# The RWKV stage of a hybrid backbone: TensorE's order written out by the program, dense work between the steps of preparation and none in the recurrence

## The chip, the core and the metric

The kernel runs on one core of a Trainium2 chip. The metric is the device time of one execution in microseconds (us), the median of several runs.

## The reference

Two layers work on 512 latent tokens and 256 context tokens of 1024 channels. A layer normalises and modulates its input to `u`, projects it, sends the parts through four mixers (RWKV-7, SSD, Hyena, retention), merges these under sigmoid gates and adds the output projection. Cut to what the change touches:

```python
for layer in range(2):
    need_ctx = layer < 1
    u_c, gate_c = modulate(h_ctx, cond_ctx, norm_w[layer], ada_w[layer], ada_b[layer])
    u_l, gate_l = modulate(h_lat, cond_lat, norm_w[layer], ada_w[layer], ada_b[layer])
    pc = split_in(u_c @ in_w[layer]); pl = split_in(u_l @ in_w[layer])
    ...   # per head of RWKV, token by token, in both directions, the context first:
        sa = -einsum('bhvk,bhk->bhv', s, kk_t)
        s = s * w_t[:, :, None, :] + sa[..., None] * b_t[:, :, None, :] + v_t[..., None] * k_t[:, :, None, :]
        y_t = einsum('bhvk,bhk->bhv', s, r_t)
    ...   # u, mod = cond @ ada_w + ada_b; merge: sum over m of sigmoid(u @ merge_w_m) * (ys_m @ branch_w_m)
```

The second layer needs no outputs for the context tokens.

## The kernel before

**Dense work.** A projection of 128 output channels (`dense`, L209) multiplies a weight block of 1024 x 128 with `u`. For accuracy `u` and the weights are held as a high and a low part, and three products are summed: `uh,whi`, `ul,whi`, `uh,wlo`. The tokens are cut in 512 (`dl`) and 256 (`dc`). Weights come by DMA (`wraw`), ACT casts the high part (`whi`, L185), VectorE subtracts it (`wlo`, L186), three buffers each. `stream` runs a list of such projections and parks their results in DRAM; it serves all mixers, and some of it convolves or gates on VectorE (L413, L711, L712).

**RWKV** (`rwkv`, `rwkv_ct`) goes through four blocks of 128 channels (two heads). A block has a *preparation*: an elementwise chain on VectorE, head sums, then for each direction d the matmuls `AR,KB` whose results VectorE masks into `A` (L577), the transposes of `KB` and the values to `KBt` and `vt`. Then comes the *inverse* of 48 triangular 32x32 blocks on VectorE: four transposes of `A` (L618), 60 small operations (L622, L623), six transposes (L627, L629) into `TT`. TensorE multiplies these with `A` and `late` in 32x32 pieces, and ACT copies the results into `TT`.

Then the *recurrence* goes through 12 chunks of 64 tokens, both directions in one tile. A step is: `UV,A` and `Z,AR` into one PSUM tile, an ACT copy to `Rs` (L669), `Rs,TT`, an ACT copy to `UV` (L675), `UV,KBt`, and two VectorE operations that add the old state and multiply by the decay `pcm` to the new state `Z` (L684, L685). The outputs (`AR,Z` and `A,UV` into `yl`) hang on that. GpSimd clears half of `UV` (L655), copies the values into it (L657) and makes `pcm` (L659). A group norm, the bonus and a gate end the block.

**Order.** A scheduler sets the order of every engine's queue. It takes the dense matmuls that stand after a block in the program into whatever holes it sees: they lie between the steps of the recurrence as well. TensorE's order, like every other engine's, is fixed when the program is built; an instruction that isn't ready holds up all that stand behind it.

**After RWKV** come the rest of the projections, Hyena, SSD, retention, then `merge` for each mixer. The modulation of the next layer (`ada_load`, `ada_step`, 64 weight pieces) runs eight pieces per output column inside the last merge of the first layer.

## Time and profile before

| | |
|---|---|
| median of 3 runs | 3047.11 us (3041.41 to 3059.58) |
| profiled execution | 3056.07 us, span 3054.3 us |
| TensorE busy | 2872.5 us (94%) |
| VectorE, ScalarE (ACT), GpSimd (POOL) busy | 1952.7 (64%), 1162.8 (38%), 446.8 us (15%) |
| mean granted TensorE clock | 0.968 |
| RWKV stages | 200 to 850 us and 1860 to 2515 us of the span |
| modulation of layer 2 | inside 1470 to 1655 us |

PE is TensorE, DVE is VectorE, POOL is GpSimd. Granted clock 1.00 is 2.4 GHz, 0.50 is 1.2 GHz. A matmul's time in the profile covers its run through the pipeline, so the starts of neighbours tell what one costs. An engine's idle time is charged to what ended it.

### The profile page before, as it was taken

To read this page: it belongs to the slowest core of one execution; us is meant where nothing else is said; L and a number is where in the kernel's file an instruction comes from. 1 tells how busy PE (TensorE), PEld (TensorE's weight loads), DVE (VectorE), ACT (ScalarE), POOL (GpSimd) and SP (SyncE) were. 2 spreads that over 40 slices of the span, in tenths; PEclk is the share of its full clock that TensorE was granted. 3 is DMA by queue.
4 is the path that set the end of the run, shared out by engine and by line. 5 is a ranking of instruction groups with operands and counts; after the bars stand their busy time and mean duration, and the time that the engine had idled before them with its cause. 6 is when DMAs were issued, how large, how long until landed. Compare 5 with 4: busy or idle time off the path is not lost. (4 is left out here: it accounts for less than half of the span.)

```text
span 3054.3 us, 48430 instructions
## 1 busy us (share of the span) xinstructions
PE 2872.5 (94%) x18708; PEld 2311.2 (76%) x18708; DVE 1952.7 (64%) x3576; ACT 1162.8 (38%) x2087; POOL 446.8 (15%) x650
## 2 busy tenths in 40 slices
PE   8998989999999999999998999898999999999897
PEld 3786777777788888778866868776777778877677
DVE  3469494949332778877466446959494825787865
ACT  4653243334232223344344454434252323333432
POOL 2311202020100001210120231120202020011111
PEclk9999999999999999999998979999999999999999
DMA  5642121212153332134256254323132225332334
GB/s 192 206 146 80 61 99 58 89 47 70 48 184 114 123 114 91 58 130 142 90 181 211 89 168 151 103 80 101 51 107 68 73 71 177 125 119 87 126 120 144
DMA packets 164266, 343.24 MB, mean 112 GB/s; under 512 B 19105, under 2 KB 28130, under 8 KB 164036
## 3 DMA queue, kind: packets, MB, share of 16 engines
q1 hardware_dynamic: 164036, 340.15, 33.9%
q8 instruction: 147, 2.41, 0.3%
q14 instruction: 83, 0.68, 0.1%
HBM read 254.77 MB, written 83.74 MB: 111 GB/s over the span
## 5 line engine op out<-in xcount | busy, mean ns | idle before, releaser
L209 PE MATMUL dl<-uh,wlo 128*128 128x512 f32 (+1 forms) x1520 | 620.9, 409 | 16.2 <-DVE wlo L186 16.1
L209 PE MATMUL dl<-uh,whi 128*128 128x512 f32 (+1 forms) x1520 | 620.2, 408 | 8.2 <-ACT xp L257 7.0
L209 PE MATMUL dl<-ul,whi 128*128 128x512 f32 (+1 forms) x1520 | 624.0, 411 | 2.0 <-DVE ul L363 2.0
L186 DVE TENSOR_TENSOR wlo<-wraw,whi 128x512 fp32r<-128x512 f32 x452 | 326.1, 722 | 336.9 <-ACT whi L185 298.6
L185 ACT CAST whi<-wraw 128x512 fp32r<-128x512 f32 x452 | 278.2, 616 | 628.6 <-PE dc L209 325.3
L209 PEld LDWEIGHTS dl<-uh,wlo 128*128 128x128 f32 (+1 forms) x1520 | 290.8, 191 | 82.6 <-DVE wlo L186 20.6
L209 PEld LDWEIGHTS dl<-uh,whi 128*128 128x128 f32 (+1 forms) x1520 | 290.0, 191 | 65.7 <-ACT xp L257 7.5
L209 PEld LDWEIGHTS dl<-ul,whi 128*128 128x128 f32 (+1 forms) x1520 | 290.0, 191 | 61.6 <-DVE ul L363 5.6
L209 PE MATMUL dc<-uh,whi 128*128 128x256 f32 (+1 forms) x960 | 279.0, 291 | 16.3 <-ACT xp L257 7.1
L209 PE MATMUL dc<-ul,whi 128*128 128x256 f32 (+1 forms) x960 | 276.7, 288 | 2.2 <-DVE ul L363 2.2
L209 PE MATMUL dc<-uh,wlo 128*128 128x256 f32 (+1 forms) x960 | 275.9, 287 | 0.0
L209 PEld LDWEIGHTS dc<-uh,whi 128*128 128x128 f32 (+1 forms) x960 | 182.4, 190 | 34.2 <-ACT xp L257 9.9
L209 PEld LDWEIGHTS dc<-ul,whi 128*128 128x128 f32 (+1 forms) x960 | 182.5, 190 | 19.1 <-DVE ul L363 6.2
L209 PEld LDWEIGHTS dc<-uh,wlo 128*128 128x128 f32 (+1 forms) x960 | 182.0, 190 | 3.5 <-issue 0.6
L1208 POOL TENSOR_TENSOR acc<-acc,fg 128x512 f32<-128x512 f32 x72 | 95.1, 1329 | 511.4 <-DVE fg L1207 511.4
L684 DVE TENSOR_TENSOR Z<-cc,Z 128x256 f32<-128x256 f32 x80 | 33.9, 424 | 203.9 <-PE cc L174 203.9
L655 POOL MEMSET UV<- 64x256 f32 x96 | 29.4, 306 | 674.5 <-PE yl L174 374.9
L814 POOL TENSOR_TENSOR m<-smask,adl 128x512 fp32r<-128x512 f32 x24 | 34.1, 1419 | 590.3 <-DVE adl L186 463.3
L669 ACT COPY Rs<-cc 64x256 f32<-64x256 f32 x96 | 35.2, 367 | 197.6 <-PE cc L174 196.9
L209 PE MATMUL dl<-yh,whi 128*128 128x512 f32 x256 | 103.3, 405 | 3.2 <-ACT yh L185 2.1
L209 PE MATMUL dl<-yl,whi 128*128 128x512 f32 x256 | 102.9, 404 | 3.1 <-DVE yl L186 3.1
L209 PE MATMUL dl<-yh,wlo 128*128 128x512 f32 x256 | 103.9, 407 | 0.0
(411 smaller groups left out, 5828.7 us busy)
## 6 DMA issues: line engine op xcount, KB each, us to landing
wraw<-in_w SPq DMA_DIRECT2D x248, 256.0 KB, 2.7
wraw<-merge_w SPq DMA_DIRECT2D x128, 256.0 KB, 2.8
adr<-ada_w SPq DMA_DIRECT2D x96, 256.0 KB, 3.6
wraw<-branch_w SPq DMA_DIRECT2D x64, 256.0 KB, 2.7
wraw<-out_w SPq DMA_DIRECT2D x32, 256.0 KB, 3.6
pdlw<-fg SPq DMA_DIRECT2D x16, 384.0 KB, 2.6
pdla<-fg SPq DMA_DIRECT2D x16, 384.0 KB, 2.9
hfd<-Hs SPq DMA_DIRECT2D x16, 384.0 KB, 2.3
```

The source lines that it names most:

```text
L185: (heng or self.S).copy(out=hi, in_=src) if heng is None else heng.tensor_copy(out=hi, in_=src)
L186: (leng or self.V).tensor_tensor(out=lo, in0=src, in1=hi.bitcast(F32), op=ALU.subtract)
L209: self.P.matmul(out[t0][:M, :n], w[:, kk, :], u[:, k, t0:t0 + n], start=(k == 0 and p == 0), stop=(k == nk - 1 and p == 2))
L655: G.memset(UV[hb], 0.0)
L669: S.copy(out=Rs[hb], in_=Rp.t[hb])
L684: V.tensor_tensor(out=Zn[:], in0=Zp.t[:], in1=Z[:], op=ALU.add)
L814: eng.tensor_tensor(out=m2[:], in0=self.smask[:, d, :].unsqueeze(1).to_broadcast([128, 4, 128]), in1=ad[:, c, hs:hs + 4].bitcast(F32).unsq ...
L1208: G.tensor_tensor(out=acc[:, oc, t0:t0 + n], in0=acc[:, oc, t0:t0 + n], in1=g[:, t0:t0 + n], op=ALU.add)
```

## The change

1. **TensorE's order.** The RWKV stage of both layers runs with TensorE's order as the program writes it (`manual_schedule`). `fill(us)` places dense chunks worth so many us (12 matmuls of n columns count 12 n / 2260) between steps of the preparation: 5, then 17 or 11, four times 1.6, four times 1.4, 4, 34, twice 1.4 and 4 per block, 89.8 us in all. `require` brings in what a block needs. What is left runs after the fourth block.
2. **Recurrence.** There is no dense work in it. Every step works on one direction and then the other: `Z`, `Rs`, the copy to `UV` and the state operations are half as wide and twice as many. The outputs of a step come one step later, and the products with the values (`from_v`) one step earlier. `UV` is no longer cleared.
3. **Inverse.** One transpose of all 128 partitions makes `TT`, and one makes `TB` (the tile `et`); they take the place of six of 32 partitions. Two ACT copies and two GpSimd memsets follow the first.
4. **Weights.** In the lead and RWKV stages of both layers GpSimd and not VectorE subtracts the high part (256 of 452 subtractions).
5. **Modulation.** Two pieces run per output column in all four merges of the first layer.
6. The light projections (`rv` to `zs`) now come before Hyena's, whose results are convolved on VectorE.

```diff
-    PSUM_A = dict(cc=3, yl=1, d1=1)
+    PSUM_A = dict(cc=4, yl=1)
...
-            self.split(hi[:], lo[:], raw[:])
+            self.split(hi[:], lo[:], raw[:], leng=self.wl)
         return hi, lo
...
@@ -207,6 +209,12 @@
                     k = j * 4 + kk
                     for p, (w, u) in enumerate(((hi, uh), (hi, ul), (lo, uh))):
                         self.P.matmul(out[t0][:M, :n], w[:, kk, :], u[:, k, t0:t0 + n], start=(k == 0 and p == 0), stop=(k == nk - 1 and p == 2))
+                yield 12 * n / 2260
...
-        m = self.tile(self.fpool, [n, 512], F32, "fg")
+        m = self.tile(self.apool, [n, 512], F32, "am")
         self.S.copy(out=m[:], in_=self.adps[:])
-        pc = self.ps("dc", [128, 4, 2])
+        pc = self.ps("s" if "s" in self.pb else "cc", [128, 4, 2])
...
+    def fill(self, us):
+
+        self.credit += us
+        while self.credit > 0:
+            c = next(self.feed, None)
+            if c is None:
+                return
+            self.credit -= c
+
+    def require(self, nm, j):
+        while (nm, j) not in self.parked:
+            self.credit -= next(self.feed)
+
...
+        self.feed = self.stream_steps(l, need_ctx, items)
+        self.credit = 0
         for ct in range(4):
             y, no = self.rwkv_ct(l, ct, need_ctx, pa, pb, segs, osegs)
-            self.stream(l, need_ctx, items[ct])
+            self.require("ga", ct)
...
+        for _ in self.feed:
+            pass
...
     def rwkv_ct(self, l, ct, need_ctx, pa, p, segs, osegs):
         V, S, G = self.V, self.S, self.G
+        for nm in "krv":
+            self.require(nm, ct)
...
+        self.fill(5)
...
+            self.fill(11 if d else 17)
+            nf = 0
...
                     pp = [self.ps("cc", [128, 4, 128]) for h in range(2)]
+                    nf += 1
+                    if nf > 2:
+                        self.fill(1.6)
...
             kt = self.tile(p, [128, 12, 128], F32, "KBt", bufs=2)
+            self.fill(1.4)
             for g in range(3):
...
+            self.fill(1.4)
...
+        self.fill(4)
         cb = self.headsum(ksum, osegs)
...
-        G.memset(TT[32:64, :, 0:32], 0.0)
-        G.memset(TT[96:128, :, 0:32], 0.0)
         for par in range(2):
             for blk in range(2):
...
+
+        V.transpose(out=TT[:, :, 0:32].rearrange("p u t -> p t u"), in_=B)
         for par in range(2):
-            V.transpose(out=TT[qs[par, 0], :, 32:64].rearrange("p u s -> p s u"), in_=B[qs[par, 0]].rearrange("p t s -> p s t"))
-            for blk in (1, 0):
-                V.transpose(out=TT[qs[par, blk], :, blk * 32:blk * 32 + 32].rearrange("p u t -> p t u"), in_=B[qs[par, blk]])
+            S.copy(out=TT[qs[par, 1], :, 32:64], in_=TT[qs[par, 1], :, 0:32])
+            G.memset(TT[qs[par, 1], :, 0:32], 0.0)
+        TB = self.tile(p, [128, 32, 32], F32, "et")
+        V.transpose(out=TB[:].rearrange("p u s -> p s u"), in_=B.rearrange("p t s -> p s t"))
         X = self.tile(p, [128, 24, 32], F32, "late")
+        self.fill(34)
         for d in range(2):
             ps = self.ps("cc", [128, 12, 32])
...
-                    self.mm(ps, ps.t[qs[par, 1], u, :], A[qs[par, 0], par * 24 + d * 12 + u, 32:64], TT[qs[par, 0], 8 * par + d * 12 + u, 32:64])
+                    self.mm(ps, ps.t[qs[par, 1], u, :], A[qs[par, 0], par * 24 + d * 12 + u, 32:64], TB[qs[par, 0], 8 * par + d * 12 + u, :])
...
         for d in range(2):
             ps = self.ps("cc", [128, 12, 32])
+            if d == 0:
+                self.fill(1.4)
...
+        self.fill(1.4)
         y = self.tile(p, [128, T], F32, "y")
+        Z = UVp = Yp = None
...
+        def from_v(c):
+            par = c % 2
+            hb, hk = slice(64 * (1 - par), 64 * (1 - par) + 64), slice(64 * par, 64 * par + 64)
+            ps = self.ps("cc", [128, 4, 64])
+            for d in range(2):
+                for h in range(2):
+                    self.mm(ps, ps.t[hb, d * 2 + h, :], A[hk, at(c, d, h), 0:64], vt[d][hk, [(c + 8) % 12, c][d] // 2, 64 * h:64 * h + 64])
+            return ps
+
+        def inner(c, uv):
+            for d in range(2):
+                for h in range(2):
+                    ao = A[:, at(c, d, h), 127:63:-1] if d else A[:, at(c, d, h), 64:128]
+                    self.mm(Yp, Yp.t[64 * h:64 * h + 64, nat(c, d):nat(c, d) + 64], uv[:, d, h, :], ao)
+
+        Rp = from_v(0)
         for c in range(12):
+            outs = c >= 4 or need_ctx
             if c == 4 or c == 0 and need_ctx:
...
             UV = self.tile(p, [128, 2, 2, 64], F32, "UV")
-            G.memset(UV[hb], 0.0)
             for d in range(2):
                 G.tensor_copy(out=UV[hk, d], in_=vt[d][hk, slot[d] // 2, :].rearrange("p (h x) -> p h x", h=2))
...
-            Rp = self.ps("cc", [128, 4, 64])
+            Rs = self.tile(p, [128, 4, 64], F32, "Rs")
             for d in range(2):
-                for h in range(2):
-                    idx = par * 24 + d * 12 + h * 6 + slot[d] // 2
-                    self.mm(Rp, Rp.t[hb, d * 2 + h, :], A[:, idx, 0:64], UV[:, d, h, :])
...
+                if Z is not None:
+                    self.mm(Rp, Rp.t[hb, 2 * d:2 * d + 2, :].rearrange("p h x -> p (h x)"), ar[d][:, slot[d], 0, :], Z[d][:])
+                S.copy(out=Rs[hb, 2 * d:2 * d + 2], in_=Rp.t[hb, 2 * d:2 * d + 2])
+            if outs and Z is not None:
                 for d in range(2):
-                    self.mm(Rp, Rp.t[hb, 2 * d:2 * d + 2, :].rearrange("p h x -> p (h x)"), ar[d][:, slot[d], 0, :], Z[:, d, :])
-            Rs = self.tile(p, [128, 4, 64], F32, "Rs")
-            S.copy(out=Rs[hb], in_=Rp.t[hb])
+                    self.mm(Yp, Yp.t[:, nat(c, d):nat(c, d) + 64], Z[d][:], ar[d][:, slot[d], 1, ::-1] if d else ar[d][:, slot[d], 1, :])
             Up = self.ps("cc", [128, 4, 64])
...
                     self.mm(Up, Up.t[hb, d * 2 + h, :], TT[hb, lane, :], Rs[hb, d * 2 + h, :])
-            S.activation(out=UV[hb].rearrange("p d h x -> p (d h) x"), in_=Up.t[hb], func=AF.Copy, scale=-1.0)
+                S.activation(out=UV[hb, d], in_=Up.t[hb, 2 * d:2 * d + 2], func=AF.Copy, scale=-1.0)
+            if UVp is not None:
+                inner(c - 1, UVp)
+            UVp = UV if outs else None
             if c < 11:
                 Zp = self.ps("cc", [128, 2, 128])
+                Zn = []
                 for d in range(2):
                     self.mm(Zp, Zp.t[:, d, :], kbt[d][:, slot[d], :], UV[:, d].rearrange("p h x -> p (h x)"))
-                Zn = self.tile(p, [128, 2, 128], F32, "Z")
-                if Z is None:
-                    V.tensor_tensor(out=Zn[:], in0=Zp.t[:], in1=pcm[:], op=ALU.mult)
-                else:
-                    V.tensor_tensor(out=Zn[:], in0=Zp.t[:], in1=Z[:], op=ALU.add)
-                    V.tensor_tensor(out=Zn[:], in0=Zn[:], in1=pcm[:], op=ALU.mult)
...
-                    if Z is not None:
-                        self.mm(Yp, Yp.t[:, nat:nat + 64], Z[:, d, :], rho)
...
-                        self.mm(Yp, Yp.t[hr, nat:nat + 64], UV[:, d, h, :], ao)
-            Z = Zn
...
+                    zn = self.tile(p, [128, 128], F32, f"Z{d}", bufs=2)
+                    if Z is None:
+                        V.tensor_tensor(out=zn[:], in0=Zp.t[:, d], in1=pcm[:, d], op=ALU.mult)
+                    else:
+                        V.tensor_tensor(out=zn[:], in0=Zp.t[:, d], in1=Z[d][:], op=ALU.add)
+                        V.tensor_tensor(out=zn[:], in0=zn[:], in1=pcm[:, d], op=ALU.mult)
+                    Zn.append(zn)
+                Z = Zn
+                if c == 3 and need_ctx:
+                    inner(c, UVp)
+                    UVp = None
+                    S.copy(out=y[:, 512:768], in_=Yp.t[:])
+                Rp = from_v(c + 1)
+        inner(11, UVp)
+        self.fill(4)
...
+            light = some(rv=4, rk=4, rq=4, gr=4, gh=4, zs=4)
+            items = []
+            for c in range(4):
+                items += [(n, c + 1) for n in "krv" if c < 3] + [("ga", c)] + light[6 * c:6 * c + 6]
+            items += [("hy", 4 * j + c) for c in range(4) for j in range(3)] + some(dt=1, x=4, B=2, C=2)
             adas = [(l, j, k) for l, j0 in ((0, 4), (1, 0)) for j in range(j0, 6) for k in range(8)]
...
+                self.wl = self.G
...
-                        with pool(f"ra{l}") as pa:
-                            with pool(f"rw{l}") as p:
-                                self.rwkv(l, need, pa, p, items)
                         nmg = 0 if need else 2
-                        self.stream(l, need, rest + [("mg", 24 + j) for j in range(nmg)])
+                        with tc.manual_schedule(engines={mybir.EngineType.PE}), pool(f"ra{l}") as pa, pool(f"rw{l}") as p:
+                            self.rwkv(l, need, pa, p, items + [("mg", 24 + j) for j in range(nmg)])
...
+                self.wl = self.V
...
-                    self.merge(l, 0, need, mp, acc, True)
-                    self.merge(l, 2, need, mp, acc, False)
-                    self.stream(l, need, [("mg", 24 + j) for j in range(nmg, 8)])
-                    self.merge(l, 1, need, mp, acc, False)
                     with pool(f"ada{l}") as self.apool:
-                        q = []
+                        q, todo = [], list(adas) if need else []
 
                         def each(oc):
-                            for a in adas[8 * oc:8 * oc + 8]:
-                                q.append(self.ada_load(*a))
-                                if len(q) > 2:
+                            for _ in range(2):
+                                if todo:
+                                    q.append(self.ada_load(*todo.pop(0)))
+                                if q and (len(q) > 2 or not todo):
                                     self.ada_step(*q.pop(0))
 
-                        self.merge(l, 3, need, mp, acc, False, True, each if need else None)
-                        for a in q:
-                            self.ada_step(*a)
+                        self.merge(l, 0, need, mp, acc, True, each=each)
+                        self.merge(l, 2, need, mp, acc, False, each=each)
+                        self.stream(l, need, [("mg", 24 + j) for j in range(nmg, 8)])
```

On TensorE, inside a recurrence step of the first block, this stands before (`Z,AR`, `Rs,TT` and so on as above, `dl` and `dc` dense):

```order
L174 MATMUL cc_2036<-UV_2015,KBt_1635 128x128
L174 MATMUL cc_2036<-UV_2015,KBt_1727 128x128
L174 MATMUL yl_1953<-A_1570,UV_2015 64x64 x2
L174 MATMUL yl_1953<-AR_1680,Z_2006 128x64
L174 MATMUL yl_1953<-A_1570,UV_2015 64x64 x2
L174 MATMUL cc_2054<-UV_2048,A_1570 64x64 x4
L209 MATMUL dl_4770<-uh_141,wlo_948_4805 128x512
L209 MATMUL dl_4770<-uh_141,whi_947_4804 128x512
L209 MATMUL dl_4770<-ul_142,whi_947_4804 128x512
L209 MATMUL dl_4770<-uh_141,wlo_948_4805 128x512
L209 MATMUL dc_4771<-uh_141,whi_947_4804 128x256
```

and this after, where `Z_541` and `Z_542` are the states of the two directions and `vt,A` is `from_v`:

```order
L174 MATMUL cc_2712<-vt_1892,A_1622 64x64 x2
L174 MATMUL cc_2712<-vt_2132,A_1622 64x64 x2
L174 MATMUL cc_2712<-Z_541_2707,AR_1639 64x128
L174 MATMUL cc_2712<-Z_542_2710,AR_1930 64x128
L174 MATMUL yl_2689<-AR_1639,Z_541_2707 128x64
L174 MATMUL yl_2689<-AR_1930,Z_542_2710 128x64
L174 MATMUL cc_2729<-Rs_2722,TT_2207 64x64 x4
L174 MATMUL yl_2689<-A_1622,UV_2690 64x64 x4
L174 MATMUL cc_2740<-UV_2717,KBt_1873 128x128
L174 MATMUL cc_2740<-UV_2717,KBt_2099 128x128
```

Two dense runs of four or more per step are gone, and the output products of the step before stand between `Rs,TT` and `UV,KBt`.

On TensorE, after the change, at the end of `fill(34)` in the first block (`et,A` is `TB` times `A`, the first product that needs the inverse's result):

```order
L211 MATMUL dl_2525<-uh_141,wlo_525_2530 128x512
L211 MATMUL dl_2525<-uh_141,whi_524_2529 128x512
L211 MATMUL dl_2525<-ul_142,whi_524_2529 128x512
L211 MATMUL dl_2525<-uh_141,wlo_525_2530 128x512
L174 MATMUL cc_2545<-et_2278,A_1622 32x32 x24
L174 MATMUL cc_2572<-et_2278,A_1622 32x32 x24
L211 MATMUL dc_2526<-uh_141,whi_524_2529 128x256
L211 MATMUL dc_2526<-ul_142,whi_524_2529 128x256
```

and on GpSimd, around the memset of that block's `TT`, which must wait for ACT's copy of the first transpose:

```order
L186 TENSOR_TENSOR wlo_516_2464<-wraw_514_2461,whi_515_2463 128x512
L186 TENSOR_TENSOR wlo_519_2494<-wraw_517_2491,whi_518_2493 128x512
L671 MEMSET TT_2207 32x32x32 x2
L186 TENSOR_TENSOR wlo_525_2530<-wraw_523_2527,whi_524_2529 128x512
L186 TENSOR_TENSOR wlo_532_2668<-wraw_530_2665,whi_531_2667 128x512
L186 TENSOR_TENSOR wlo_635_3143<-wraw_633_3140,whi_634_3142 128x512
```

The memset stands ahead of the subtraction for `wlo_525`, with which the last matmuls of `fill(34)` work.

On VectorE, after the change, inside the inverse of the fourth block (L663 and L664 are its small operations, L779 and L780 the convolution of a Hyena projection):

```order
L664 TENSOR_TENSOR KB_7033<-KB_7033 128x19x12
L663 TENSOR_TENSOR KB_7033<-KB_7033 128x234
L779 SCALAR_TENSOR_TENSOR fg_7150<-xp_60_157,cols_48_121,fg_7150 128x512
L664 TENSOR_TENSOR KB_7033<-KB_7033 128x18x13
L780 SCALAR_TENSOR_TENSOR fg_7150<-xp_60_157,cols_48_121,fg_7150 128x512
L663 TENSOR_TENSOR KB_7033<-KB_7033 128x238
L779 SCALAR_TENSOR_TENSOR fg_7150<-xp_60_157,cols_48_121,fg_7150 128x256
L664 TENSOR_TENSOR KB_7033<-KB_7033 128x17x14
L780 SCALAR_TENSOR_TENSOR fg_7150<-xp_60_157,cols_48_121,fg_7150 128x256
L663 TENSOR_TENSOR KB_7033<-KB_7033 128x240
L664 TENSOR_TENSOR KB_7033<-KB_7033 128x16x15
L663 TENSOR_TENSOR KB_7033<-KB_7033 128x240
```

The subtractions that stood inside the inverse are gone from VectorE; evictions of dense results stand in it as before.

## Rows read from the trace of the kernel before

**Rows 1.** Windows of both RWKV stages: start, length, busy of five engines, granted clock, DMA.

```profile
200.00:850.00 650.00, 610.52 (x4876) 492.54 (x4875) 451.04 (x775) 236.53 (x436) 98.49 (x215) 0.96 0.22 72
1860.00:2515.00 655.00, 611.88 (x4564) 479.78 (x4564) 439.40 (x754) 240.13 (x438) 102.71 (x220) 0.96 0.26 85
```

**Rows 2.** Waits of TensorE, first stage (200–850): total us, times, longest us.

```profile
PE cc L174 <- DVE TT L627: 16.9, 7, 4.6
```

**Rows 3.** Waits of TensorE, second stage (1860–2515).

```profile
PE cc L174 <- DVE TT L627: 16.8, 7, 6.0
PE dl L209 <- DVE wlo L186: 12.8, 7, 4.3
```

**Rows 4.** Windows, matmuls of line 209 alone: length, busy and count, clock.

```profile
200.00:850.00 650.00, 379.08 (x1806) 0.96 0.22 72
304.80:371.10 66.30, 29.64 (x120) 1.00 0.18 61
...
1860.00:2515.00 655.00, 398.22 (x1672) 0.96 0.26 85
...
2439.80:2501.60 61.80, 29.80 (x119) 1.00 0.15 50
```

**Rows 5.** Groups of VectorE by line, whole program: busy, mean ns.

```profile
L623 DVE TENSOR_TENSOR KB<-KB 128x30 f32<-128x30 f32 (+14 forms) x240 | 82.2, 342 | 3.6
L622 DVE TENSOR_TENSOR KB<-KB 128x30 f32<-128x30 f32 (+14 forms) x240 | 79.9, 333 | 3.9
L618 DVE STREAM_TRANSPOSE KB<-A 32x1024 f32<-32x1024 f32 x32 | 64.3, 2009 | 2.7 <-PE cc L174 2.4
L629 DVE STREAM_TRANSPOSE TT<-KB 32x1024 f32<-32x1024 f32 x32 | 62.3, 1947 | 0.9
```

**Rows 6.** Timeline of TensorE before a TT matmul: start, us, instruction, [idle <- releaser].

```profile
2293.42 0.39 PE L209 MATMUL dl<-uh,wlo 128*128 128x512 f32 x1
2293.65 0.40 PE L209 MATMUL dl<-uh,whi 128*128 128x512 f32 x1
2296.27 1.70 PE L174 MATMUL cc<-TT,A 32*32 32x32 f32 x92 [2.22 <-DVE TT L627]
```

**Rows 7.** Timeline of one recurrence step: start, us, instruction.

```profile
2470.82 0.65 PE L174 MATMUL cc<-Z,AR 128*64 128x128 f32 x4
...
2471.57 0.37 ACT L669 COPY Rs<-cc 64x256 f32<-64x256 f32 x1 [3.58 <-PE cc L174]
...
2473.92 0.61 PE L174 MATMUL cc<-UV,KBt 128*128 128x128 f32 x4
...
2474.57 0.42 DVE L684 TENSOR_TENSOR Z<-cc,Z 128x256 f32<-128x256 f32 x1 [0.61 <-PE cc L174]
...
2475.26 0.63 PE L174 MATMUL cc<-UV,A 128*64 128x64 f32 x8
```

**Rows 8.** Groups of VectorE by shape, whole program.

```profile
L577 DVE TENSOR_TENSOR A<-cc,maska 128x128 f32<-128x128 f32 x32 | 8.6, 285 | 5.8 <-PE cc L174 5.8
```

**Rows 9.** Groups of GpSimd by shape, whole program.

```profile
L814 POOL TENSOR_TENSOR m<-smask,adl 128x512 fp32r<-128x512 f32 x24 | 34.1, 1419 | 590.3 <-DVE adl L186 463.3 <-PE s L174 127.0
```

**Rows 10.** Timeline inside an inverse, VectorE and GpSimd.

```profile
275.63 0.69 DVE L186 TENSOR_TENSOR wlo<-wraw,whi 128x512 fp32r<-128x512 f32 x1
...
277.11 0.41 DVE L623 TENSOR_TENSOR KB<-KB 128x238 f32<-128x238 f32 x1
277.14 1.28 POOL L420 TENSOR_TENSOR fg<-xp 128x512 f32<-128x512 f32 x1 [9.79 <-ACT xp L257]
...
277.55 1.12 DVE L622 TENSOR_TENSOR KB<-KB 128x234 f32<-128x234 f32 x1
```

**Rows 11.** Waits of TensorE while the modulation runs (1470–1660).

```profile
PE sy L303 <- DVE adl L186: 7.4, 12, 1.3
```

**Rows 12.** Windows of all engines in three stretches.

```profile
1625.00:1660.00 35.00, 26.91 (x95) 14.76 (x96) 22.38 (x37) 21.30 (x35) 2.34 (x2) 0.66 0.68 212
2158.00:2186.00 28.00, 28.00 (x226) 18.21 (x227) 6.54 (x14) 6.83 (x16) 8.49 (x23) 1.00 0.10 30
2298.00:2311.80 13.80, 13.80 (x138) 10.66 (x139) 9.07 (x13) 5.97 (x12) 1.17 (x3) 0.51 0.38 125
```

More of the change, by code (lines that the diff above doesn't have):

```diff
@@ L196, in weights, with dense_steps @@
         with self.tc.high_priority(offset=500):
-            self.split(hi[:], lo[:], raw[:])
+            self.split(hi[:], lo[:], raw[:], leng=self.wl)
         return hi, lo
-    def dense(self, srcs, uh, ul, segs, M=128):
-        out = {t0: self.pst("dl" if n > 256 else "dc", [128, n]) for t0, n in segs}
+    def dense_steps(self, out, srcs, uh, ul, segs, M=128):
+        for t0, n in segs:
+            out[t0] = self.pst("dl" if n > 256 else "dc", [128, n])
         nk = len(srcs) * 4
@@ L209, in dense @@
                         self.P.matmul(out[t0][:M, :n], w[:, kk, :], u[:, k, t0:t0 + n], start=(k == 0 and p == 0), stop=(k == nk - 1 and p == 2))
+                yield 12 * n / 2260
+    def dense(self, srcs, uh, ul, segs, M=128):
+        out = {}
+        for _ in self.dense_steps(out, srcs, uh, ul, segs, M):
+            pass
         return out
@@ L387, in apply_gate, with stream_steps @@
         self.V.scalar_tensor_tensor(out=y[:, :no], in0=g[:, :no], scalar=0.5, in1=y[:, :no], op0=ALU.mult, op1=ALU.mult)
+    def fill(self, us):
[8 more added lines that the diff above has]
+            self.credit -= next(self.feed)
     def stream(self, l, need_ctx, items):
+        for _ in self.stream_steps(l, need_ctx, items):
+            pass
+    def stream_steps(self, l, need_ctx, items):
         V, S, G = self.V, self.S, self.G
@@ L407, in stream @@
             M = 16 if nm == "dt" else 128
-            ps = self.dense([src[:, 0:4], src[:, 4:8]], self.uh, self.ul, sg, M)
+            ps = {}
+            yield from self.dense_steps(ps, [src[:, 0:4], src[:, 4:8]], self.uh, self.ul, sg, M)
             g = fg()
@@ L697, in rwkv_ct @@
-            Z = Zn
-            if c == 3 and need_ctx:
-                S.copy(out=y[:, 512:768], in_=Yp.t[:])
+                    zn = self.tile(p, [128, 128], F32, f"Z{d}", bufs=2)
[4 more added lines that the diff above has]
+                        V.tensor_tensor(out=zn[:], in0=zn[:], in1=pcm[:, d], op=ALU.mult)
@@ L1287, in run @@
             self.cond()
-            items = [[(n, c + 1) for n in "krv"] + [("ga", c)] for c in range(3)] + [[("ga", 3)]]
             def some(**kw):
                 return [(n, j) for n, c in kw.items() for j in range(c)]
-            rest = [("hy", 4 * j + c) for c in range(4) for j in range(3)] + some(gh=4, dt=1, x=4, B=2, C=2, zs=4, rq=4, rk=4, rv=4, gr=4)
+            light = some(rv=4, rk=4, rq=4, gr=4, gh=4, zs=4)
[3 more added lines that the diff above has]
+            items += [("hy", 4 * j + c) for c in range(4) for j in range(3)] + some(dt=1, x=4, B=2, C=2)
             adas = [(l, j, k) for l, j0 in ((0, 4), (1, 0)) for j in range(j0, 6) for k in range(8)]
```

30 lines of the change are left out of this document (16 added, 14 removed).

## Prediction

> **What bounds the kernel now.** I read the windows of the two RWKV stages first, since nearly all of the change lies there. Both keep TensorE busy for 94% of their time [rows 1]: 650 − 610.5 and 655 − 611.9 us are idle, 83 us together, and a granted clock of 0.96 means that 1305 x 0.04 = 52 us were lost at half speed. So some 135 us of 1305 can be had from waits and clock; the rest is matmuls and their order. The waits then: the first product with the inverse's result waits 7 times in each stage, 16.9 and 16.8 us, once 6.0 us [rows 2, 3], and in the second stage 12.8 us go to weights that VectorE had not yet split [rows 3].
>
> What fills the rest comes from counts. A steady dense matmul of 512 columns takes 0.23 us (2293.65 − 2293.42) [rows 6], one of 256 half of that. The first stage has 1806 dense matmuls [rows 4], 907 of them wide in the program's order: 907 x 0.23 + 899 x 0.115 = 312 us; the second 1672, 1216 wide: 332 us. So 338 and 323 us are not dense. The eight recurrences, of which rows 4 shows the first and the last, take 267 us with 473 dense matmuls in the first stage, and 263 us with 443 in the second. At the stage's mean cost (312/1806 and 332/1672) these are 82 and 88 us, which leaves **185 and 175 us of recurrence proper**. The remaining 153 + 148 = 301 us are preparation, **37.6 us per block**.
>
> **The change, part by part.**
>
> *Preparation.* TensorE's own small work per block: 96 `AR,KB` and 48 transposes at about 0.11 us (four such take 0.65 and 0.61, about 0.28 of it the last one's way through the pipeline [rows 7]), 15.9; 192 pieces of 32x32 at 1.70/92 us [rows 6], 3.5; head sums and norms about 4: 23.4 us. Each change from dense to small costs near 0.2 us (a run of four is 0.2 longer than four shares), eleven of them 2 us. The rest of the 37.6, some 12 us, is waiting and half clock. What waits after?
>
> The first candidate is the inverse. From the last `AR,KB` to the first product, TensorE has 1.4 + 1.4 + 4 + 34 = 40.8 us of dense work and about 6 of small. VectorE's chain in that time: masks 1.6, four transposes of 2.01, the 60 small operations (82.2 + 79.9)/8 = 20.3 [rows 5], bonus 1.1, one transpose about 2 (as L618; the 32-partition form takes 1.95 [rows 5]) and another for `TB`: 33 us to the first of them, 35 to the second. GpSimd now makes about seven splits in that time. A small operation takes 0.41 us alone and 1.12 behind a GpSimd operation of 1.28 [rows 10]: seven collisions cost 5 to 9 us; I take 7. On the other hand the splits that stood there on VectorE (0.69 [rows 10]) are gone. Chain to the first transpose: 40 us. Then the memset of `TT` must pass on GpSimd, and behind it the split for the last 2.3 us (in one block 5) of `fill(34)`, about 2.5 us more. So TensorE, with 44.5 us of work in hand, is reached at 42.5: no wait, unless evictions stand inside the inverse. They do: by the order none in the first block of each layer, then gates and convolutions worth about 2, 4 and 9 us in layer 1 and 9, 7 and 11 us in layer 2. **Waits for the inverse: about 38 us, against 33.7 before.** They don't vanish.
>
> The second candidate is the first `AR,KB` of a block, behind some 29 us of TensorE work but 31 to 35 of VectorE's, 2 us a block. Together 54 us, 6.7 per block; the bounds are 1 (no evictions in the way, no collisions) and 12 (what there is now). Preparation after: 23.4 + 2 + 6.7 = 32.1 us, **−44 us for eight blocks** (−89 to 0).
>
> *GpSimd's splits.* 256 of them at 1.42 us (nearest row: 128x512 to fp32r [rows 9]) are 363 us in stages and leads of some 1600, so its queue has room; in the lead it has 2.1 us operations ahead, for which I add **+3 us** (0 to 10). The Trainium skill ("SBUF — State Buffer", Who interferes with whom) says that a VectorE operation with two inputs in SBUF and a GpSimd operation that reads SBUF exclude each other for a whole instruction, which speaks against this move. Here the trace agrees: 277.55 + 1.12 is 0.25 us past the end of the GpSimd operation. By the full rule, with 1.42 per collision, the chain would be 10 − 7 = 3 us longer in each of the six blocks that wait, and the preparation would gain 18 us less.
>
> *Recurrence.* Now it has nothing in its holes. TensorE's step: four products of 0.11 with `Z`, four of 0.16 into `yl`, four of 0.11 with `KBt`, 24 small ones of 0.058 (0.63 for eight less the way through the pipeline [rows 7]), with the starts of runs 3.2 to 3.4 us. The chain of the later direction: VectorE now makes four operations of 0.285 (128x128 [rows 8]) instead of two of 0.42 [rows 7], one after the other, so it is some 0.4 us behind; the ACT copies shrink from 0.37 [rows 7] to about 0.26. With the latencies between engines a step is 3.3 us if the outputs hide all copies, 4.1 if none. I take 3.7, since the copies after `Z` have only 0.6 us of cover; 2.95 in the four context steps of layer 2, which have no outputs. Layer 1: 4 x (12 x 3.7 + 1.5) = 184 us against 185; layer 2: 4 x (4 x 2.95 + 8 x 3.7 + 1.5) = 172 against 175. **−4 us** (−42 to +34). The dense work pushed out isn't lost: it has been counted at 0.23 throughout.
>
> *Modulation.* In 1625–1660 TensorE is busy for 26.9 of 35 us at clock 0.66 [rows 12]: 12 us lost at half speed, and 7.4 us go to splits of the pieces [rows 11]. Spread over four merges both should shrink: **−12 us** (−19 to 0). Of the rest of the order after RWKV little moves.
>
> *Clock.* Here is what could turn it. After the wait of 2.22 us at 2294–2296 [rows 6] the stretch 2298–2311.8 runs at 0.51 although TensorE is never idle in it [rows 12] and though it still has dense matmuls between its steps. The trace shows such a fall behind the other waits for the inverse too. On the other hand the context steps at 2158–2186, with hardly any dense work, keep 1.00 [rows 12]. After the change each wait is followed by 2.3 us of dense work, twice 1.4 us among the 32x32 pieces, and then by none for 45 us. So a fall should mostly be made good before the recurrence; one that isn't lasts to its end. A step at half clock would be 5.1 to 5.4 us, bound by TensorE's own work: +17 us for a recurrence. I count **one such recurrence, +17 us, and +6 for short falls** at four waits (3 us each, half lost). The trace has no recurrence without dense work, so the bounds are none and all eight, 0 to +136. The Trainium skill ("TensorE: Matmul & The Clock Gate", What's actually happening) has the clock fall when TensorE idles and rise when it has been busy for a while; by that alone a recurrence that keeps TensorE at work would soon be back at full clock, and the sum would be 17 us lower. The stretch 2298–2311.8, busy for 13.8 us of 13.8 and still at 0.51, contradicts it, so I keep the 17.
>
> **Sum.** −44 + 3 − 4 − 12 + 17 + 6 = −34 us on the profiled 3056: 3022. The median of the runs shown lies 9 us lower than the profiled one, so the forecast is **3013 us**.
>
> **Rivals.**
>
> 1. *The waits stay whole.* VectorE's chain lengthens by what the GpSimd collisions and evictions add, and the preparation is as long as before: the −44 is gone, 3047 + 10 = **3057 us**. For it: six of eight inverses have evictions inside; against it: VectorE is rid of 256 splits.
> 2. *Recurrences at 1.2 GHz* (the other side). The place is the wait for `TB` or the short first step of a recurrence, with nothing behind it that is dense. Price 17 us each; with three fallen the gain is gone (3047), from four on it is slower than before by more than can be told: four give 3064, all eight **3132 us**. For it: the half-clock stretch above; against it: the context steps at 1.00 and the 2.8 us of dense work behind the wait.
> 3. *Waits and falls vanish.* The evictions find VectorE's idle time before the inverse, the clock holds: −54 − 23, **2936 us**; with steps of 3.3 us near 2900.
> 4. *Dense work was free in the recurrence's holes*, so pushing it out costs. At 185/48 = 3.9 us of its own in a step of 267/48 = 5.6 little hole was left; only steps of 4.1 us would make it tell, +38: 3051. I count it with rival 1.
>
> **How the numbers follow.** The forecast has 0.44 and spans 2985 to 3040; 0.15 of that is the case that no recurrence stays at half clock, 3013 − 17 = 2996. Rivals 1 and 4 have 0.17 (3040 to 3065), rival 2 has 0.23 (3050 to 3135), rival 3 has 0.16 (2900 to 2985). About half a per cent, 15 us, is what a measurement here tells from no change. Faster than 3032: 0.40 of the forecast and all of rival 3, 0.56. Within: 0.04 + 0.12 + 0.02 = 0.18. Slower than 3062: 0.05 + 0.21 = 0.26. The range 2940 to 3100 leaves out the lower part of rival 3 (0.08) and the upper of rival 2 (0.12).
>
> **What would show it.** Right: the RWKV stages with their dense tails shorter by 20 us each; steps of 3.5 to 3.9 us between `UV,KBt` and `UV,KBt`, clock 1.00 in at least six recurrences; TensorE waiting for a split on GpSimd or for `TB` at the end of `fill(34)` in the later blocks; lengthened small operations beside GpSimd's splits. Wrong: a clock of 0.5 through whole recurrences, steps above 4.1 us, waits for splits all along the preparation, or idle time at the modulation as before.

## The result, and the profile after

The changed kernel takes **3540.22 us** (median of 4 runs, 3539.09 to 3541.06) against 3050.51 for the kernel before, a ratio of 1.1605 (95% interval 1.1568 to 1.1642). It is 16% slower, far outside the range. A ratio leaves out runs that lie over 1.5% above the fastest of the same kernel; this touches one experiment, where three of six runs, near 3170 us, are left out. The profiled span is 3539.3 us, the mean granted clock 0.857 where it was 0.968.

The page's busy times and its row of the clock in 40 slices, after:

```profile
PE 3132.4 (89%) x18708; PEld 2517.4 (71%) x18708; DVE 1889.1 (53%) x3456; ACT 1204.1 (34%) x2295; POOL 754.2 (21%) x810
...
PEclk9879587695876999999999979679596785999999
```

TensorE is busy for 260 us more with the same 18708 matmuls, and the clock is down in the slices of all eight recurrences. The windows of the stages after (columns as in [rows 1]) are cut at the same places of the program as those of before below them: to the first `AR,KB`, to the first product of Hyena's transform, to the output projection, and for layer 2 from its end on.

```profile
0.00:257.00 257.00, 197.89 (x864) 139.79 (x864) 94.21 (x145) 109.80 (x190) 75.66 (x74) 0.86 0.44 147
257.00:1249.00 992.00, 876.82 (x5729) 709.76 (x5730) 443.21 (x770) 294.33 (x613) 232.57 (x279) 0.79 0.21 68
1249.00:1902.00 653.00, 630.34 (x3743) 517.52 (x3744) 461.88 (x947) 244.59 (x437) 79.66 (x62) 1.00 0.38 126
1976.00:2157.00 181.00, 133.56 (x643) 109.88 (x642) 80.91 (x100) 88.93 (x149) 71.75 (x60) 0.86 0.37 125
2157.00:3029.00 872.00, 759.39 (x4692) 592.34 (x4690) 407.28 (x709) 265.53 (x549) 227.63 (x278) 0.76 0.21 68
```

The same stretches before:

```profile
0.00:221.00 221.00, 203.06 (x1030) 144.64 (x1030) 106.50 (x174) 118.76 (x209) 60.73 (x65) 0.98 0.56 183
221.00:988.00 767.00, 728.95 (x5563) 597.19 (x5563) 466.39 (x805) 264.82 (x491) 92.53 (x210) 0.97 0.26 85
988.00:1655.00 667.00, 636.13 (x3744) 517.37 (x3745) 461.85 (x946) 247.24 (x437) 81.52 (x62) 0.99 0.38 125
1728.00:1894.00 166.00, 153.16 (x745) 120.07 (x743) 86.88 (x124) 95.06 (x161) 52.13 (x50) 0.90 0.46 151
1894.00:2558.00 664.00, 622.93 (x4599) 488.78 (x4600) 434.59 (x752) 241.06 (x440) 95.31 (x209) 0.96 0.27 90
```

The first lead grew by 36 us, the first RWKV stage with its dense tail by 225, the second lead by 15, the second stage by 208; the stretch with the modulation shrank by 14, and what follows the second stage, up to the output projection, grew by 14 (448 against 434). That is 484 of the 485 us between the spans. Not all of it is what it seems, since dense work changed places. The matmuls of `dense` in four of these stretches, after and before (columns as in [rows 4]):

```profile
0.00:257.00 257.00, 73.62 (x372) 0.86 0.44 147
257.00:1249.00 992.00, 501.76 (x2656) 0.79 0.21 68
1976.00:2157.00 181.00, 71.28 (x348) 0.86 0.37 125
2157.00:3029.00 872.00, 403.94 (x1812) 0.76 0.21 68
```

```profile
0.00:221.00 221.00, 107.72 (x538) 0.98 0.56 183
221.00:988.00 767.00, 497.35 (x2490) 0.97 0.26 85
1728.00:1894.00 166.00, 98.25 (x448) 0.90 0.46 151
1894.00:2558.00 664.00, 410.90 (x1717) 0.96 0.27 90
```

At the costs per matmul of the forecast, by width, these are 65, 458, 64 and 364 us after and 93, 429, 83 and 346 before. So without their dense work the leads grew by **64 and 34 us**, and the stages by 196 and 190, 386 us together. Of that the recurrences take nearly all. From the first product with the values to the last output they take 92, 90, 91 and 92 us in layer 1 and 86, 86, 89 and 89 in layer 2, in sum 365 and 350: 365 − 185 = 180 and 350 − 175 = 175, **355 us**. That leaves some **31 us** for the preparation. The second recurrence and the sixth:

```profile
581.00:671.00 90.00, 74.90 (x415) 0.53 0.01 5
2467.00:2553.00 86.00, 70.76 (x402) 0.52 0.03 7
```

The second recurrence, its first 6 us and the next 80; its last output ends at 671.6:

```profile
581.00:587.00 6.00, 4.03 (x34) 0.99 0.15 61
587.00:667.00 80.00, 67.38 (x358) 0.50 0.00 1
```

A step takes 8.06 us instead of 3.7. Its timeline, VectorE and ACT beside TensorE:

```profile
604.75 0.27 ACT L744 ACTIVATE UV<-cc 64x128 f32<-64x128 f32 x1 [1.41 <-PE cc L174]
...
605.08 0.69 PE L174 MATMUL cc<-Rs,TT 64*64 64x64 f32 x4 [0.36 <-ACT UV L744]
...
607.15 0.29 DVE L757 TENSOR_TENSOR Z<-cc,Z 128x128 f32<-128x128 f32 x1 [6.20 <-PE cc L174]
...
607.59 0.76 PE L174 MATMUL cc<-UV,KBt 128*128 128x128 f32 x2 [0.48 <-DVE Z L757]
...
610.73 0.26 ACT L735 COPY Rs<-cc 64x128 f32<-64x128 f32 x1 [1.33 <-PE cc L174]
...
611.05 0.69 PE L174 MATMUL cc<-Z,AR 128*64 128x128 f32 x2 [0.41 <-ACT Rs L735]
```

Each second direction's product starts just behind the copy or addition that reads the *first* direction's result: `Rs,TT` of direction 1 waits 0.36 us for ACT's copy of direction 0, `UV,KBt` 0.48 for VectorE's addition, `Z,AR` 0.41 for ACT. The two directions write halves of one PSUM tile. The chain of waits in the first stage counts it, 48 or 40 times each, with the waits of the preparation below:

```profile
PE cc L174 <- ACT UV L744: 20.0, 48, 0.9
PE cc L174 <- ACT Rs L735: 19.1, 48, 0.4
PE cc L174 <- DVE Z L757: 19.0, 40, 0.5
PE dc L211 <- ACT fg L462: 14.3, 2, 7.2
PE dc L211 <- DVE fg L439: 13.6, 6, 3.3
PE dc L211 <- ACT xp L265: 13.0, 3, 11.4
```

No wait for `TT` or `TB` is left in this stage, nor one for a split on GpSimd; in the second stage they are 2.3 and 1.3 us. In their place TensorE stands at a `dc` matmul until ACT or VectorE has emptied the one `dc` buffer (41 us in three rows). The first stage before had 12.5 us of such waits:

```profile
PE dc L209 <- ACT xp L257: 7.1, 4, 3.3
PE dc L209 <- DVE fg L413: 5.4, 1, 5.4
```

### The profile page after: what moved, and what is told of

It reads as the page before. It is cut to its first block, busy times and chain, and to the rows that moved or that the text cites. A ratio compares the mean times of both kernels' runs of the same rounds, so it can differ in the third digit from the quotient of the medians.

```text
span 3539.3 us, 48732 instructions
## 1 busy us (share of the span) xinstructions
PE 3132.4 (89%) x18708; PEld 2517.4 (71%) x18708; DVE 1889.1 (53%) x3456; ACT 1204.1 (34%) x2295; POOL 754.2 (21%) x810
## 5 line engine op out<-in xcount | busy, mean ns | idle before, releaser
L211 PE MATMUL dl<-ul,whi 128*128 128x512 f32 (+1 forms) x1520 | 613.3, 404 | 4.5 <-DVE ul L371 4.4
L186 POOL TENSOR_TENSOR wlo<-wraw,whi 128x512 fp32r<-128x512 f32 (+1 forms) x256 | 357.3, 1396 | 791.6 <-ACT whi L185 743.4
L211 PE MATMUL dc<-uh,whi 128*128 128x256 f32 (+1 forms) x960 | 290.6, 303 | 61.2 <-ACT fg L462 20.7
L757 DVE TENSOR_TENSOR Z<-cc,Z 128x128 f32<-128x128 f32 x160 | 46.6, 292 | 519.4 <-PE cc L174 519.4
L186 DVE TENSOR_TENSOR wlo<-wraw,whi 128x512 fp32r<-128x512 f32 x196 | 144.9, 740 | 91.0 <-ACT whi L185 84.4
L735 ACT COPY Rs<-cc 64x128 f32<-64x128 f32 x192 | 49.0, 259 | 391.5 <-PE cc L174 391.3
L174 PE MATMUL cc<-UV,KBt 128*128 128x128 f32 x352 | 134.8, 486 | 42.2 <-DVE Z L757 38.0
L174 PE MATMUL cc<-Rs,TT 64*64 64x64 f32 x768 | 128.6, 319 | 47.8 <-ACT UV L744 38.8
L174 PE MATMUL cc<-Z,AR 128*64 128x128 f32 x352 | 120.5, 446 | 35.1 <-ACT Rs L735 35.1
L174 PEld LDWEIGHTS cc<-Rs,TT 64*64 64x64 f32 x768 | 93.2, 207 | 79.5 <-ACT UV L744 56.5
```

The source lines that it names most:

```text
L174: i = self.P.matmul(out, lhsT, rhs, start=start, stop=True, skip_group_check=True, is_transpose=tr or None)
L186: (leng or self.V).tensor_tensor(out=lo, in0=src, in1=hi.bitcast(F32), op=ALU.subtract)
L211: self.P.matmul(out[t0][:M, :n], w[:, kk, :], u[:, k, t0:t0 + n], start=(k == 0 and p == 0), stop=(k == nk - 1 and p == 2))
L735: S.copy(out=Rs[hb, 2 * d:2 * d + 2], in_=Rp.t[hb, 2 * d:2 * d + 2])
L757: V.tensor_tensor(out=zn[:], in0=Zp.t[:, d], in1=Z[d][:], op=ALU.add)
```

## The experiments

All times are medians beside runs of the kernel before on the same chip (3042 to 3046 us), and the ratios are to these. The gains of runs on the changed kernel are told against its 3540.

**Separate PSUM tiles** for the directions.

```diff
-            ps = self.ps("cc", [128, 4, 64])
             for d in range(2):
+                ps = self.ps("cc", [128, 2, 64])
...
+                Up = self.ps("cc", [128, 2, 64])
...
+                    Zp = self.ps("cc", [128, 128])
+                    self.mm(Zp, Zp.t[:], kbt[d][:, slot[d], :], UV[:, d].rearrange("p h x -> p (h x)"))
```

> The changed kernel, but each direction of a recurrence step has PSUM tiles of its own (six products into six tiles instead of three). Theory A: TensorE's product of the second direction waits until the first direction's part of the same tile has been read (three waits of 0.36 to 0.48 us in a step), and the idling takes the clock down; without the shared tile those waits go, the clock stays at 1.00, a step takes 3.5 to 3.9 us instead of 8.06, a recurrence about 46 us instead of 85: 3540 - 8 x 39 = about 3230 us. Rival B: the clock is lost because no dense work is in the recurrence, whatever waits: it stays at 0.5, a step is twice TensorE's own 3.3 us, about 6.6: 3540 - 96 x 1.4 = about 3405 us.

3290.69 us, 1.0799 (1.0743 to 1.0856): 249 us of the loss are gone, and the time lies between the two expectations. The windows show why; these are stretches of the first, the second and the fifth recurrence:

```profile
354.00:414.00 60.00, 59.47 (x369) 0.52 0.00 1
554.00:589.00 35.00, 34.78 (x363) 1.00 0.01 2
2098.00:2153.00 55.00, 54.95 (x322) 0.50 0.01 5
```

Two of eight, both in layer 1, ran at 1.00 and six at 0.5, with the same instructions within a layer: such a stretch takes 35 us at 1.00 and 60 at 0.5 in layer 1, and 55 in layer 2. A step at 1.00 and one at 0.5:

```profile
565.88 0.65 PE L174 MATMUL cc<-Z,AR 128*64 128x128 f32 x4
...
567.04 0.68 PE L174 MATMUL cc<-Rs,TT 64*64 64x64 f32 x8
...
567.94 0.69 PE L174 MATMUL cc<-UV,KBt 128*128 128x128 f32 x4 [0.22 <-ACT UV L746]
```

```profile
376.27 1.11 PE L174 MATMUL cc<-Rs,TT 64*64 64x64 f32 x8
...
377.41 1.19 PE L174 MATMUL cc<-UV,KBt 128*128 128x128 f32 x4
```

A step takes 3.45 us at 1.00 and 5.95 at 0.5; the three waits are gone. So the shared tile is shown to cost 8.06 − 5.95 = 2.1 us a step at half clock, and the clock still falls without it in most recurrences. Both theories hold a part.

**Dense work in every step**, with the shared tiles.

```diff
                 Rp = from_v(c + 1)
+                self.fill(1.4)
```

> The changed kernel with its shared tiles, but 1.4 us of dense work put into every step, behind the products with the values of the next. Rival B: the dense work brings the clock back; a step takes 3.3 + 1.2 of waits + 0.4 + 1.4 = 6.3 us, of which 4.9 are its own: 3540 - 8 x (85 - 59) = about 3330 us. Theory A: the waits are still there and the clock is not brought back by so little: steps of 8.06 + 2.8 us at 0.5, total 3540 + 96 x 1.4 = about 3675 us.

3553.12 us, 1.1661 (1.1614 to 1.1707). The clock comes back in part,

```profile
596.00:696.00 100.00, 86.65 (x452) 0.63 0.06 19
```

and seven recurrences run at 0.57 to 0.70, but TensorE is idle for 13% of the one shown, and the time is 13 us longer than the change's. Dense work alone cures nothing while the waits are there. Neither number is met: rival B's 3330 is far off, and theory A's 3675 took the dense work as added, while it was only moved there from behind the stage.

**Both.**

> Both: tiles of its own for each direction, and 1.4 us of dense work in every step. If theory A is right the dense work has nothing left to give, and this is as fast as the run with separate tiles alone, about 3230 us with steps of 3.7 + 1.4 us. If rival B is right it is the only one of the three with a clock of 1.00: about 3230 us against 3405 and 3330.

3200.72 us, 1.0504 (1.0461 to 1.0548). The first recurrence, and the last, for which no dense work was left:

```profile
356.00:405.00 49.00, 48.51 (x436) 1.00 0.10 34
2619.00:2674.00 55.00, 54.93 (x321) 0.50 0.00 1
```

Seven recurrences run at 0.94 to 1.00. It is 90 us faster than with separate tiles alone, so B's part is shown too. With the same dense work the clock was 0.57 to 0.70 with the waits and is 0.94 to 1.00 without them, so the waits hold it down as well.

**Dense work in the first four steps alone**, separate tiles.

```diff
                 Rp = from_v(c + 1)
+                if c < 4:
+                    self.fill(1.4)
```

> Separate tiles (3291 us, two recurrences of eight at clock 1.00), and 1.4 us of dense work in the first four steps of a recurrence alone. Theory: the clock is decided in the first step, which has no products with the state and waits 0.36 and 0.50 us for the two ACT copies, and in layer 2 in the context steps, which have no outputs; once past them a step of 3.45 us holds the clock without dense work, as in two recurrences of the run before. Then nearly all recurrences show 1.00 and steps of 3.45 us after the fourth: six recurrences gain 20 us each, about 3170 to 3200 us. Rival: steps without dense work lose the clock sooner or later wherever they stand: several recurrences still end at 0.5, about 3250 to 3290 us.

3160.13 us, 1.0385 (1.0346 to 1.0425), 131 us faster than separate tiles alone and 41 faster than with dense work in every step. The last recurrence, at 0.5 in the run before:

```profile
2593.00:2636.00 43.00, 41.39 (x346) 0.91 0.09 28
```

All eight run at 0.90 or above, and nearly every step behind the fourth takes 3.45 us without any dense work. In this run the clock is lost in the first steps or not at all. Whether the dense columns hold it or the idle time that they fill is not separated.

**Subtraction back on VectorE.**

```diff
-                self.wl = self.G
+                self.wl = self.V
```

> The changed kernel with the weights' subtraction back on VectorE. If GpSimd's reads of SBUF hold up the inverse and the masks, the preparation loses some of its 70 us over before: 3480 to 3510 us. If the queue of GpSimd is not what the preparation waits for, VectorE has 256 operations of 0.7 us more and the time stays within 15 us of 3540 or grows.

3489.03 us, 1.145 (1.1405 to 1.1496): 51 us less. One of the two groups of VectorE's small operations, in the changed kernel and in this one:

```profile
L663 DVE TENSOR_TENSOR KB<-KB 128x30 f32<-128x30 f32 (+14 forms) x240 | 107.4, 448 | 7.4
```

```profile
L663 DVE TENSOR_TENSOR KB<-KB 128x30 f32<-128x30 f32 (+14 forms) x240 | 80.4, 335 | 6.5
```

With the other group (99.0 and 81.2 us) it is 206 us against 162, which is what it was [rows 5]: GpSimd's splits made the inverse 45 us longer in eight blocks, 5.6 us each. That is not yet the 51 us, since hardly anything waited for the inverse's end in the changed kernel. What did get shorter in the first stage are TensorE's waits for the emptied `dc` buffer: the three rows of 41 us above are 24 us here (9.7, 14.0 and 0.2). The rest is spread over the whole program: the first recurrence starts 10 us earlier, the last 43.

**Leads filled**: both repairs of the recurrence, VectorE's subtraction, and six light projections handed to the scheduler; four and six more merge gates take their place in the stages.

```diff
-                        nmg = 0 if need else 2
+                        nmg = 4 if need else 8
+                        self.stream(l, need, light[:6])
```

> The kernel with separate tiles and 1.4 us of dense work per step (3201 us), with the subtraction back on VectorE, and with six light projections of each layer put under the scheduler, ahead of the RWKV stage, so that they can fill the holes of the lead; four more merge gates (layer 1) and six more (layer 2) are brought into the stage in their place. Theory: the leads lose 64 and 34 us over before because the written order keeps all later dense work out of them; with work to fill in they give back some 60 of the 98, the subtraction gives 50 as in its own run, and the last recurrence of layer 2 has dense work and keeps the clock: 3201 - 60 - 50 - 10 = about 3080 us. Rival: the leads are long because GpSimd has more in its queue there and the waits are those of Hyena's filters: only the 50 come back, about 3150 us.

3092.8 us, 1.0161 (1.0128 to 1.0195): 108 us less than with both repairs, 57 beyond the subtraction's 51, near the 60 expected of the leads. The first lead now holds 660 dense matmuls instead of 372 in nearly the same time:

```profile
0.00:254.00 254.00, 130.46 (x660) 0.98 0.51 170
```

The last recurrence still had no dense work and ran at 0.5, and with VectorE's chain longer the wait for `TB` came up: 38.4 us in four pieces.

**All four repairs** (dense work in the first four steps).

> The written order with all four repairs: separate tiles, dense work in the first four steps of a recurrence, VectorE's subtractions, six light projections per layer under the scheduler ahead of the stage. If the causes found add up: 3160 - 51 (subtraction) - 57 (what the leads gave back beside it) = about 3050 us, the time of the kernel before. Rival: they overlap, since VectorE's subtractions lengthen its chain to the first product with TB (38 us of waits there in the run with the leads filled): 3080 to 3110 us.

3050.09 us, 1.0014 (0.9983 to 1.0046): the sum of 3050 is met, and the written order ends where the kernel before was. One repair did not hold everywhere, though. In the profile the last recurrence runs at half clock to its end, with 21 dense matmuls in its first steps:

```profile
2474.00:2548.00 74.00, 73.91 (x395) 0.50 0.04 13
```

Just ahead of it TensorE waits 1.49 us for `TB` and 0.86 us for ACT's copy of `late`, and the clock is at 0.50 from 2470 us on, before the first step. That is the other place that rival 2 had named. The other seven run at 0.89 or above. So the exact sum is in part luck: a recurrence at 0.5 costs some 25 us.

**The scheduler's order** with separate tiles, and the rest of the change.

```diff
-                        with tc.manual_schedule(engines={mybir.EngineType.PE}), pool(f"ra{l}") as pa, pool(f"rw{l}") as p:
+                        with pool(f"ra{l}") as pa, pool(f"rw{l}") as p:
```

> The changed kernel with separate tiles, but TensorE's order left to the scheduler as before; all else of the change stays (alternating directions, merged transposes, GpSimd's subtractions, the modulation spread). Theory: the written order itself costs what is left beside the recurrence's tiles (the leads, the waits of the preparation for one eviction, the dense-free steps): 3040 to 3090 us, clock 0.95 or above in the recurrences. Rival: half as wide and twice as many operations in the recurrence make the chain longer whatever the order: above 3150 us.

3105.62 us, 1.0203 (1.0146 to 1.0261), of two runs 25 us apart: between the expectations, nearer the theory. It is 185 us less than with separate tiles in the written order, so that order costs a good deal, but the alternating form isn't at 3050 without it.

**The same with VectorE's subtraction and no dense work placed by hand.**

> The changed kernel without its first and fourth part: the order is the scheduler's and no dense work is placed by hand, VectorE subtracts; directions alternate in separate tiles, transposes merged, modulation spread. It differs from the kernel before with merged transposes and spread modulation (3003 us) by the alternating recurrence and the order of the projections. Theory: with the scheduler's dense work in its holes the recurrence's own time hardly matters, so it is within 15 us of 3003. Rival: TensorE's own work is less in it (3.45 us a step against some 3.9), which gives up to 96 x 0.4 = 38 us: about 2965; or the many small operations push evictions back: about 3040.

3084.82 us (three runs, 3084.74 to 3088.3), 1.0143 (1.0105 to 1.0182). None of the expected numbers is met. Why it is 82 us behind the kernel before with the same transposes and modulation (below, 3003) stays open; no trace shows these three runs.

**The modulation alone**, on the kernel before.

> The kernel before with the fifth part of the change alone: the modulation's pieces two per output column in all four merges. The forecast's term was -12 us, and in the trace of the changed kernel the stretch from Hyena to the output projection of layer 1 is 14 us shorter: 3046 - 12 = about 3034 us. Rival: the pieces' subtractions on VectorE hold up the other merges instead: no change.

3025.55 us, **0.9944** (0.9925 to 0.9964), 17 us faster than its neighbour's 3043. Of the wait of 7.4 us in [rows 11] 1.1 is left.

**The modulation and the merged transposes**, on the kernel before.

```diff
-            V.transpose(out=TT[qs[par, 0], :, 32:64].rearrange("p u s -> p s u"), in_=B[qs[par, 0]].rearrange("p t s -> p s t"))
...
+        V.transpose(out=TT[:, :, 0:32].rearrange("p u t -> p t u"), in_=B)
```

> The kernel before with the modulation spread and the third part of the change: one transpose of 128 partitions and TB in the place of six of 32 partitions. Theory: VectorE's chain to the first product with TT is 8 us shorter in each block, the waits for it (33.7 us in the two stages) go for the greater part and the falls of the clock behind them with them: 30 us less than with the modulation alone, about 3005 us. Rival: the scheduler puts evictions into the time that is won, and the waits stay: within 10 us of the run with the modulation alone.

3003.05 us, **0.9858** (0.9829 to 0.9888), as expected in time, but not for the reason given. TensorE's waits with the modulation alone, and with both:

```profile
PE cc L174 <- DVE TT L627: 33.1, 15, 5.7
PE dl L209 <- DVE wlo L186: 14.4, 9, 3.9
...
PE dl L209 <- ACT xp L257: 7.3, 1, 7.3
PE dc L209 <- ACT xp L257: 7.3, 4, 3.2
```

```profile
PE cc L174 <- DVE et L629: 34.0, 8, 6.4
...
PE dl L209 <- DVE wlo L186: 3.1, 2, 2.4
```

The wait for the inverse is as long as it was (33.1 and 34.0 us, in 15 and 8 pieces). What went are the waits for weights and for ACT's copies of dense results (`xp`), and VectorE has 53 us less to do in the two stages; that the one comes of the other is read from these rows and was not tried by itself. It is the fastest version found, with the next one.

**Light projections first**, added to that.

> The kernel before with merged transposes and spread modulation (3003 us), and with the sixth part: the light projections ahead of Hyena's. Theory: fewer convolutions stand inside VectorE's inverse in the first blocks, so the waits for TB (34 us in that run) shrink: about 2990 us. Rival: they come back in the later blocks and ahead of Hyena's own stage, which then waits for its inputs: 3003 us or more.

3002.45 us, 0.9853 (0.9823 to 0.9883): no difference from the run before. The rival's time was met, and the wait for `TB`, 39.0 us where it was 34.0, didn't shrink as the theory had it; the rest of the rival's reason is not shown.

## Why the prediction was wrong

**The recurrence is the step that failed**, in two of its sentences. The chain of a step was added up as if each direction waited only for its own inputs, and "a step is 3.3 us if the outputs hide all copies, 4.1 if none" was given as its bounds. The product of the second direction waits until the first one's part of the same PSUM tile has been read, three times a step; the program showed the shared `Rp`, `Up` and `Zp`, and I did not ask what a tile in two halves means for the order of its readers and writers. The changed kernel's step is 8.06 us; with separate tiles it is 3.45 us at 1.00, near the 3.7 of the forecast, so the rest of that sum was right. Both signs named for being wrong came: a clock of 0.5 through whole recurrences and steps above 4.1 us.

**The clock** was the second step that failed. The forecast counted one recurrence at half clock for 17 us; all eight were, and with the waits each lost some 44. The place was named by rival 2, "the short first step of a recurrence, with nothing behind it that is dense"; its price of 17 us, at most 136 in all, was for steps without the shared tile: with separate tiles the step at 0.5 is 5.95 us where the forecast had 5.1 to 5.4, and the same 363 matmuls take 59 − 35 = 24 us more. The two parts strengthen one another: with the waits the same dense work leaves the clock at 0.57 to 0.70, and at half clock the matmuls between the waits take longer. The 355 us came of that. 249 went with the tiles and another 131 with dense work in four steps, 380 together. In that last run the eight recurrences take 390 us, some 41 of them dense at the stage's mean cost, so about 350 of their own where the kernel before has 360.

**The preparation** was forecast at −44 us and gave about +31. The waits for the inverse, counted at 38 us (by the forecast's own terms, 2 us in hand against evictions of 2 to 11, it is 30), were 2, where before they were 33.7. Those for the emptied buffers of dense results were not counted: in the two stages they are 71 us where they were 20. In a written order TensorE stands at the next dense chunk until the eviction of the last has passed the queues of ACT and VectorE. That this is the cause is read from the rows; a second `dc` buffer would have had to come from `cc`, and it was not tried. The second candidate, the first `AR,KB` of a block, was counted at 16 us; the waits for `KB` and the masks are 32 us where they were 6, and those for weights 1 where they were 16. By these waits alone the stages are 32 us longer, near the 31.

**GpSimd's splits** were given 3 us and seven collisions a block. The collisions were sized well (5.6 us a block against 7), but the whole costs 51 us by its own run, and only in part where the forecast had looked.

**The leads** were left out of the sum but for those 3 us. The written order begins with the stage, so the scheduler can no longer draw its dense work forward: 64 and 34 us. The first lead holds 372 dense matmuls where it held 538, the second 348 where it held 448; the forecast counted those of the stages alone.

**The modulation** was right: −12 forecast, −14 in the trace, −17 by its own run. The merged transposes, whose gain I had put into the waits for the inverse, are worth 22 us through VectorE's other work.

**On rules.** The stretch of [rows 12] was rightly held against the Trainium skill's statement that "activity releases the throttle" ("TensorE: Matmul & The Clock Gate", What's actually happening): in the run with separate tiles TensorE is busy for 54.95 of 55 us and stays at 0.50. The profile's busy time counts a matmul's whole way through the pipeline, so it doesn't show how much of the array worked.

## What to carry to other kernels

When an operation on two independent halves is split so that they can alternate, split its PSUM tile too, and look in the order for a writer of one half behind a reader of the other. Before dense work is taken out of a serial stage, ask what holds the clock in its first steps; here four steps' worth held the clock at 0.90 or above in all eight recurrences of one run and at 0.89 or above in seven of eight of another, and with none six of eight lost it. Look also at the wait just ahead of the stage: the eighth lost its clock there. A hand-written order takes work away from whatever lay ahead of it as well: count the work per stretch before and after, the stretches outside the edit included.

## What was not expected of the hardware

The same recurrence has two lasting states: with separate tiles, 363 matmuls take 35 us at 1.00 or 59 us at 0.5, and without dense work none of the six that fell got back to 1.00 before its end. Steps of 3.45 us, which have TensorE busy for 34.78 of 35 us with small matmuls alone, keep 1.00; once at 0.5 the same steps, busy for 59.47 of 60 us, do not get back. Dense matmuls between the small ones are no sure way back: in the run with all four repairs the last recurrence has 21 of them and stays at 0.50 for 74 us, busy for 73.91.
